# A hybrid decoder step in three-product fp32r: sample tokens' x and B are turned to tokens once, and the sample states of four sequences grow in one group of four matmuls on row strips of TensorE, with some orders beside it rewritten

## The chip, the core and the metric

The kernel runs on one core of a Trainium2 chip. A core has a matrix engine (TensorE, PE in the profile, with PEld for its weight loads), a vector engine (VectorE, DVE), an activation engine (ScalarE, ACT), a general engine (GpSimd, POOL) and a queue engine (SyncE, SP) that here only issues DMAs. Each takes its own list of instructions strictly in order; semaphores tie the lists together. The metric is the device time of one execution in microseconds (us), as a median over runs.

## The reference

One layer of a hybrid decoder works on 256 prompt tokens (one sequence) and 64 sample tokens (eight sequences of eight), 320 columns in all:

```python
h = rms_norm(x, norm_mix_pre);  proj = h @ w_in          # 2048 -> 9248
gate, v   = chunk_spatial_gate(proj[u], proj[v], ...)    # gMLP heads, chunks of 128
xBC       = silu(causal_conv(proj[xBC], conv_state))     # x: 32 heads x 64, B and C: 4 groups x 128
dt        = softplus(proj[dt] + dt_bias); a = -exp(a_log)
# SSD:  h_t = exp(dt_t a) h_{t-1} + dt_t x_t B_t^T,   y_t = h_t C_t  (per head; B, C per group of 8 heads)
x = x + rms_norm([gate || norm(y * silu(z))] @ w_out, norm_mix_post)
up = causal_conv(rms_norm(x, norm_ffn_pre) @ w_up);  g, u = split(up)
x = x + rms_norm((gelu(g) * u) @ w_down, norm_ffn_post)
```

Among the outputs are the SSD states after the step. For each of the eight sample sequences and 32 heads the new state is the old 64 x 128 state times the sequence's total decay plus the sum over its eight tokens of (decay to the end x dt x x) times B. Per sequence and group of eight heads this is a sum over eight tokens that makes 128 x 512 numbers: eight sequences and four groups, 32 such growths.

## The kernel before

**Main work.** Activations lie feature-major (features on partitions, 320 tokens along the row). An fp32 product is made of three fp32r matmuls: activations and weights are each split in a high and a low part, and `accumulate` (L139) adds whi·hi (L141), whi·lo (L142) and wlo·hi (L143) for every 128 x 128 weight block, each 320 columns wide. Weights come in slabs of 1024 columns, 512 KB and eight blocks, 24 matmuls (`slab`, L118): SP loads `wraw` (L124, three buffers), ACT casts it to `whi` (L128, three buffers), DVE subtracts for `wlo` (L130, three buffers). The order of a kernel's time is: input projection with the gMLP and SSD heads between its slabs (to about 806 us), the handover to the FFN, then the FFN in up and down parts.

**Who sets the order.** A scheduler simulates the program and sorts each engine's list by priority. Slabs have high priority. Work beside them is written as Python generators (tasks in the background), which get one step ("tick") for each part of a slab, so that a `yield` moves what follows it by a slab or a part of one. `tc.issue_after(ins)` keeps what stands in it behind a named instruction in the order; it is no wait on the chip beyond the data's own.

**To tokens.** The SSD heads need x and B with tokens on partitions. `by_token` (L382) turns a 128 x 128 piece by a matmul against the identity. For the group's B: `bt_ps`, 16 pieces; for each of four groups' x: `xt_ps`, 16 pieces. Of the four banks of four pieces, two hold the prompt (banks 0, 1). The other two hold sample tokens fourfold: `fourfold` (ACT copies, L390) writes each half of the 64 sample tokens four times side by side, so that the turned piece has them at four places on the partitions. From these DVE makes `xdt` and `xq` (`times`, L800), and ACT sends `xq` to DRAM (`xq_d`). The decay rows `dt` and `dec` have five column groups for this: two for the prompt, one for the 64 samples, two for the fourfold halves (`dt_ps` L473, `dec_ps` L539).

**Growing the sample states** (`renewals`, L1150) runs in the background of the FFN, from 927 to 1318 us. For each group g it loads `xsp` from `xq_d`, splits it, and then goes over i = 0..3: ACT makes `bm`, the B rows masked by `bsel` to one sequence (the other rows zero); two states (h = 0, 1) are loaded, scaled by POOL (`tote`), grown by one matmul of all 128 rows each (`up_ps`, L1202, 512 columns), added by DVE (L1203) and sent out by ACT's queue (L1207). A state's buffer `st` is one of four.

**The handover to the FFN.** After the last slab of the output projection, `rsqrt_by_root` makes the norm's factor `r2b` (`spread`, L290). `x1_ready` (L1034) then makes for each of 16 feature tiles on DVE: scale (L1039), add x (L1040), and the split for the next product, `h_hi` by ACT (L370) and `h_lo` by DVE (L371). PE needs `h_hi` and `h_lo` of tile 0, then of 1, and so on. In the same stretch ACT copies the prompt's final states out of PSUM (L1017, L1044), and POOL adds them (L1162). DVE then sums the squares (`sq3`, L300) for the next norm, and PE turns these to `tsum` (L282).

**The decay masks.** For each head group ACT makes `cs` by a Relu (L896) and an Exp from a row that a DMA spreads (`cs<-dacs_d`, L792); `xs`, the SiLU of the convolved x, is made by ACT too (L428, L429) and is what the transposes `xt_ps` wait for.

Of the kernel before, what the change touches and what calls it, by code (L numbers as in the profile page):

```python
# [34 lines left out]
def hybrid_step(  # L35
# [38 lines left out]
    bsel = cp.tile([P, 4], F32, name="bsel")  # L74
# [4 lines left out]
    def masks():  # L79
# [7 lines left out]
        for r in range(4):  # L87
            rs = slice(32 * r, 32 * r + 32)
            pool.tensor_copy(bsel[rs], bd2[rs, rs].rearrange("p (b t) -> p b t", b=4)[:, :, 0])
# [13 lines left out]
    def col(i):  # L103
        return prm[:, i:i + 1]
# [228 lines left out]
    xq_d = dr.tile([4, P, 2, 512], F32, name="xq_d")  # L333
    bsp_d = dr.tile([P, 2, 512], F32, name="bsp_d")
# [28 lines left out]

    def split(hi, lo, x, scale=None):

        if scale is None:
            act.copy(hi, x)
            dve.tensor_tensor(out=lo, in0=x, in1=hi.bitcast(F32), op=ALU.subtract)
        else:
            made = act.activation(hi, x, AF.Copy, scale=scale).ins  # L370
            dve.scalar_tensor_tensor(out=lo, in0=x, scalar=scale, in1=hi.bitcast(F32), op0=ALU.mult, op1=ALU.subtract)  # L371
            return made
# [13 lines left out]

    def fourfold(out, x):

        for i in range(2):
            act.copy(out[:, :, i], x[:, :, 32 * i:32 * i + 32].unsqueeze(2).to_broadcast([P, 4, 4, 32]))  # L390
        return out.rearrange("p k i q t -> p k (i q t)")

    with ExitStack() as mctx:
# [47 lines left out]
        dt = op.tile([P, 5, NH], F32, name="dt")  # L441
        sda = op.tile([P, 3, NH], F32, name="sda")
        dec = op.tile([P, 5, NH], F32, name="dec")
# [4 lines left out]
        def dt_columns(xf, pre):  # L448
# [15 lines left out]
            for i in range(2):  # L464
                pool.tensor_copy(dtf[:, (3 + i) * P:(4 + i) * P].rearrange("p (q t) -> p q t", q=4),
                                 dtf[:, NP + 32 * i:NP + 32 * i + 32].unsqueeze(1).to_broadcast([P, 4, 32]))

        def steps():
# [3 lines left out]
            for c in range(5):  # L472
                pe.matmul(ps[:, NH * c:NH * c + NH], dtf[:, P * c:P * c + P], heads4, start=True, stop=True)  # L473
            H5 = 5 * NH
            dve.tensor_tensor(out=dt, in0=ps[:, :H5].rearrange("p (c h) -> p c h", c=5),
                              in1=bias_bc.unsqueeze(1).to_broadcast([P, 5, NH]), op=ALU.add)

            e = op.tile([P, 5, NH], F32, name="sp_e")
            q = dec
            z2 = tp.tile([P, NT], F32, tag="pv", name="sp_z2", bufs=4)[:, :5 * NH].rearrange("p (c h) -> p c h", c=5)  # L480
            act.activation(e, dt, AF.Abs)
# [11 lines left out]
            dve.scalar_tensor_tensor(out=dt, in0=dt, scalar=0.0, in1=q, op0=ALU.max, op1=ALU.add)  # L493
# [3 lines left out]
            dve.scalar_tensor_tensor(out=da, in0=dt, scalar=-1.0, in1=ea.unsqueeze(1).to_broadcast([P, 5, NH]),  # L497
# [36 lines left out]
            later_s = tp.tile([P, NT], F32, tag="pv", name="later_s", bufs=4)[:NS, :2 * P].rearrange("p (r q t) -> p r q t", r=2, q=4)  # L534
            for r in range(2):
                rs = slice(32 * r, 32 * r + 32)
                pool.tensor_tensor(out=later_s[:, r], in0=later[:NS, rs].unsqueeze(1).to_broadcast([NS, 4, 32]),
                                   in1=bd[:, rs].unsqueeze(1).to_broadcast([NS, 4, 32]), op=ALU.mult)
                pe.matmul(ps[:, (3 + r) * NH:(4 + r) * NH], later_s[:, r].rearrange("p q t -> p (q t)"), da[:NS, 2],  # L539
                          start=True, stop=True)  # L540
            act.activation(dec.rearrange("p c h -> p (c h)"), ps[:, :H5], AF.Exp)
            dve.tensor_tensor(out=dt[:, 3:5], in0=dt[:, 3:5], in1=dec[:, 3:5], op=ALU.mult)
# [207 lines left out]
        with tc.tile_pool(name="sd", bufs=1) as sd:  # L750
            btok = sd.tile([P, 2, 512], F32, name="btok")

            bsp = sd.tile([P, 2, 512], F32R, name="bsp")
# [4 lines left out]
            x4 = fourfold(sd.tile([P, 4, 2, 4, 32], F32, tag="x4", name="b4", bufs=1), bT[:, :, NP:NT])  # L758
            for c in range(4):
                ps = misc("bt_ps")  # L760
                for g in range(4):
                    by_token(ps[:, P * g:P * g + P], (bT if c < 2 else x4)[:, g], c % 2)
                if c < 2:
                    act.copy(btok[:, c, :], ps)
                else:
                    b = bsp[:, c - 2]
                    act.copy(b, ps)
                    for rs in (slice(32, 64), slice(96, P)):
                        dve.tensor_tensor(out=b[rs], in0=ps[rs], in1=b[rs].bitcast(F32), op=ALU.subtract)
            act.dma_start(bsp_d, bsp.bitcast(F32))  # L770
# [4 lines left out]
            def ssd(g):  # L775
# [26 lines left out]
                x4 = fourfold(sd.tile([P, 4, 2, 4, 32], F32, tag="x4", name="x4", bufs=1), xs[:, :, NP:NT])  # L802
                turned = []
                yield
                for c in range(4):
# [3 lines left out]
                    for j in range(4):  # L809
                        by_token(ps[:, P * j:P * j + P], (xs if c < 2 else x4)[:, j], c % 2)  # L810
                    if c < 2:
                        times(xdt[:, c, :], ps, c)
                    else:
                        turned.append(ps)
                xq = sd.tile([P, 2, 512], F32, tag="x4", name="xq", bufs=1)
# [572 lines left out]
```

## Time and profile before

| what | value |
|---|---|
| median of 3 runs | 1770.68 us (1770.61 to 1771.82) |
| the profiled execution | 1769.41 us |
| its span | 1767.7 us |
| TensorE clock granted | 1.0 of full, every slice |
| PE busy | 1758.7 us (99%), 12207 instructions |
| DVE / ACT / POOL busy | 1163.9 (66%) / 815.9 (46%) / 266.5 us (15%) |
| DMA | 303.35 MB, mean 172 GB/s |

The page lists instructions by line, engine, operation and tile. Matmuls on PE overlap, so a matmul's listed time (310 ns for 320 columns) is longer than the interval at which they follow each other; intervals are read from start to start in the timeline. The chain of work that ended last is traced back from the last instruction. In a row of the timeline, the brackets give the idle time of that engine before the instruction and what ended it.

### The profile page before, as it was taken

The page shows a single profiled execution, that of the slowest core. Times are in us where ns is not written, and L with a number is a line of the kernel's source. Part 1 is how long each engine was busy: PE and PEld are TensorE (multiplying, and loading weights), DVE is VectorE, ACT ScalarE, POOL GpSimd, SP SyncE. Part 2 cuts the span into 40 slices and gives each one's busy share as a digit, 9 for nine tenths or more (in the row PEclk, how much of TensorE's full clock was granted, in tenths as well). Part 3 has the DMA queues.
Part 4 walks back from the last instruction along what each step waited for, and adds up shares of the span by engine and source line. Part 5 has one row for each costly group of instructions (what it writes and reads, how often), then busy time and mean ns, then how long its engine had stood idle before and what let it go on. Part 6 is the DMA issues. An engine that isn't in the chain of part 4 may idle for free.

```text
span 1767.7 us, 31184 instructions
## 1 busy us (share of the span) xinstructions
PE 1758.7 (99%) x12207; PEld 1737.5 (98%) x12207; DVE 1163.9 (66%) x1956; ACT 815.9 (46%) x1201; POOL 266.5 (15%) x596
## 2 busy tenths in 40 slices
PE   9999999999999999999999999999999999999998
PEld 9999999999999999998999999999999999999998
DVE  7349754657767576678865666676767565656575
ACT  7344545333754544445545434343434343333335
POOL 1003210000111001022321312021101010111004
PEclk9999999999999999999999999999999999999999
DMA  7455544445665644444656656556554444444443
GB/s 253 137 179 182 172 156 150 156 155 191 226 210 161 209 144 138 158 161 145 195 177 200 209 177 204 191 184 210 183 180 157 146 156 146 156 152 148 156 147 107
DMA packets 228691, 303.35 MB, mean 172 GB/s; under 512 B 19552, under 2 KB 150720, under 8 KB 228352
## 3 DMA queue, kind: packets, MB, share of 16 engines
q1 hardware_dynamic: 216560, 281.27, 49.7%
q10 hardware_dynamic: 10448, 15.57, 2.4%
q0 software_dynamic: 1536, 4.52, 1.0%
q8 instruction: 96, 1.57, 0.4%
q14 instruction: 51, 0.42, 0.1%
HBM read 283.47 MB, written 17.58 MB: 170 GB/s over the span
## 4 chain that ended last, share of the span: by engine, by line
PE 98%; DVE 1%; DMA 0%; ACT 0%; issue 0%; POOL 0%; DVEq 0%; ACTq 0%
PE ps L141 21%; PE ps L143 21%; PE ps L142 21%; PE pd L141 10%; PE pd L143 10%; PE pd L142 10%; PE y_ps L910 1%; PE yo_ps L859 0%; PE up_ps L1202 0%; PE sg L714 0%; PE tsum L282 0%; PE xt_ps L382 0%; PE vt_ps L599 0%; PE early L70 0%; PE s_ps L841 0%; DMA cs<-dacs_d 0%
## 5 line engine op out<-in xcount | busy, mean ns | idle before, releaser
L130 DVE TENSOR_TENSOR wlo<-wraw,whi 128x1024 fp32r<-128x1024 f32 x470 | 585.5, 1246 | 409.3 <-ACT whi L128 406.8
L128 ACT CAST whi<-wraw 128x1024 fp32r<-128x1024 f32 x470 | 492.3, 1048 | 705.2 <-PE ps L142 432.8
L141 PE MATMUL ps<-h_hi,whi 128*128 128x320 f32 x2528 | 782.7, 310 | 0.5 <-ACT h_hi L370 0.5
L142 PE MATMUL ps<-h_lo,whi 128*128 128x320 f32 x2528 | 780.7, 309 | 1.4 <-DVE h_lo L371 1.4
L143 PE MATMUL ps<-h_hi,wlo 128*128 128x320 f32 x2528 | 779.9, 309 | 0.0
L142 PEld LDWEIGHTS ps<-h_lo,whi 128*128 128x128 f32 x2528 | 475.2, 188 | 2.6 <-DVE h_lo L371 1.9
L141 PEld LDWEIGHTS ps<-h_hi,whi 128*128 128x128 f32 x2528 | 474.9, 188 | 2.6 <-ACT h_hi L370 1.3
L143 PEld LDWEIGHTS ps<-h_hi,wlo 128*128 128x128 f32 x2528 | 474.7, 188 | 0.2
L141 PE MATMUL pd<-fhi,whi 128*128 128x320 f32 x704 | 217.3, 309 | 0.0
L143 PE MATMUL pd<-fhi,wlo 128*128 128x320 f32 x704 | 217.3, 309 | 0.0
L142 PE MATMUL pd<-flo,whi 128*128 128x320 f32 x704 | 217.3, 309 | 0.0
L141 PE MATMUL pd<-ohi,whi 128*128 128x320 f32 x448 | 139.5, 312 | 0.0
L143 PE MATMUL pd<-ohi,wlo 128*128 128x320 f32 x448 | 138.7, 310 | 0.0
L142 PE MATMUL pd<-olo,whi 128*128 128x320 f32 x448 | 138.6, 309 | 0.0
L142 PEld LDWEIGHTS pd<-flo,whi 128*128 128x128 f32 x704 | 132.1, 188 | 0.7
L143 PEld LDWEIGHTS pd<-fhi,wlo 128*128 128x128 f32 x704 | 132.1, 188 | 0.0
L141 PEld LDWEIGHTS pd<-fhi,whi 128*128 128x128 f32 x704 | 132.1, 188 | 0.0
L234 DVE TENSOR_TENSOR acc_ffn<-acc_ffn,pd 128x320 f32<-128x320 f32 x160 | 76.9, 482 | 32.3 <-PE pd L143 31.1
L141 PEld LDWEIGHTS pd<-ohi,whi 128*128 128x128 f32 x448 | 84.0, 188 | 1.9 <-ACT cs L897 0.8
L142 PEld LDWEIGHTS pd<-olo,whi 128*128 128x128 f32 x448 | 84.1, 188 | 0.2 <-issue 0.2
L143 PEld LDWEIGHTS pd<-ohi,wlo 128*128 128x128 f32 x448 | 84.1, 188 | 0.0
L1094 POOL COPY ptf<-pad 128x2 f32<-128x2 f32 x88 | 21.9, 250 | 406.0 <-DVE pad L1082 405.5
(303 smaller groups left out, 1546.5 us busy)
## 6 DMA issues: line engine op xcount, KB each, us to landing
wraw<-in_ffn_w_up SPq DMA_DIRECT2D x176, 512.0 KB, 3.5
wraw<-in_w_in SPq DMA_DIRECT2D x142, 512.0 KB, 3.5
wraw<-in_ffn_w_down SPq DMA_DIRECT2D x88, 512.0 KB, 3.3
wraw<-in_w_out SPq DMA_DIRECT2D x64, 512.0 KB, 3.3
st<-in_state_ssm SPq DMA_DIRECT2D x64, 256.0 KB, 4.5
out_ssm_state_sample<-st ACTq DMA_DIRECT2D x32, 256.0 KB, 2.7
cs<-dacs_d SPq DMA_DIRECT2D x16, 320.0 KB, 5.9
xr<-in_xT SPq DMA_DIRECT2D x4, 640.0 KB, 5.3
```

Of the source, the lines that this page charges most:

```text
L128: act.copy(hi[:, :m], raw[:, :m])
L130: dve.tensor_tensor(out=lo[:, :m], in0=raw[:, :m], in1=hi[:, :m].bitcast(F32), op=ALU.subtract)
L141: pe.matmul(ps, whi, xhi, start=first, stop=False)
L142: pe.matmul(ps, whi, xlo, start=False, stop=False)
L143: newest[0] = pe.matmul(ps, wlo, xhi, start=False, stop=last).ins
L234: dve.tensor_tensor(out=acc[:, nb, :], in0=acc[:, nb, :], in1=ps[:, :NT], op=ALU.add)
L910: pe.matmul(ps[64 * i:64 * i + 64, cols], w(hl), x(hl, m, cpx), tile_position=(0, 64 * i), **flags)
L1094: pool.tensor_copy(ptf[:, k, :], pad[:, 256:258])
```

## The change

1. **To tokens once.** `fourfold` and its buffers are gone. Samples' B and x are turned once: of the third bank, B in four pieces 64 tokens wide, x in two pieces 128 tokens wide (the last 128 columns, for tokens on the upper partitions) and two 64 wide; the fourth bank is gone. The result goes to one DRAM array `xb_d` (x and B of the 64 tokens, per group).
2. **Fewer decay rows.** `dt` has three turned groups where there were five, `dec` four; the matmul for the fourfold rows (L539) is one where it was two.
3. **Row strips.** Per group, 16 small DMAs bring each sequence's eight tokens of x and B to four places in a strip of 32 partitions (`tokens`). ACT copies the rounded high parts, and DVE makes the low parts by two masked operations with `low` (a constant of -1 and 0, made at the start in place of `bsel`). A strip thus holds hi·hi, hi·lo, lo·hi and lo·lo of eight tokens. Four matmuls then stand in a row, each on 32 rows of the array at `tile_position=(32*i, 0)` and each into a PSUM bank of its own: four sequences' states. Two such groups (h = 0, 1) per g, eight in all. States are loaded four at once; those of h = 1 lie in buffers `s1` and `x1d` that the SSD part has left.
4. **Relu later.** The decay masks' Relu stands behind the last SiLU (`issue_after(last_silu)`); in group 2 the transposes come one tick later.
5. **The handover.** In `x1_ready`, scale, add and split have an order of their own, so that `h_lo` of tile 0 stands before the work of later tiles; POOL's adds of the final states (and their outputs) stand behind a small POOL copy that reads the last tile of x1.

```diff
-            x4 = fourfold(sd.tile([P, 4, 2, 4, 32], F32, tag="x4", name="b4", bufs=1), bT[:, :, NP:NT])
-            for c in range(4):
+            for c in range(3):
                 ps = misc("bt_ps")
+                n = P if c < 2 else NS
                 for g in range(4):
-                    by_token(ps[:, P * g:P * g + P], (bT if c < 2 else x4)[:, g], c % 2)
+                    pe.transpose(ps[:n, P * g:P * g + P], bT[:, g, P * c:P * c + n], ident)
...
-                x4 = fourfold(sd.tile([P, 4, 2, 4, 32], F32, tag="x4", name="x4", bufs=1), xs[:, :, NP:NT])
-                turned = []
-                yield
-                for c in range(4):
+                yield from repeat(None, 2 if g == 2 else 1)
+                for c in range(3):
...
-                        by_token(ps[:, P * j:P * j + P], (xs if c < 2 else x4)[:, j], c % 2)
+                        if c < 2:
+                            by_token(ps[:, P * j:P * j + P], xs[:, j], c)
+                        else:
+                            n = P if j < 2 else NS
+                            pe.transpose(ps[:n, P * j:P * j + P], xs[:, j, NT - n:NT], ident)
...
-            for c in range(5):
+            for c in range(3):
                 pe.matmul(ps[:, NH * c:NH * c + NH], dtf[:, P * c:P * c + P], heads4, start=True, stop=True)
...
-                pe.matmul(ps[:, (3 + r) * NH:(4 + r) * NH], later_s[:, r].rearrange("p q t -> p (q t)"), da[:NS, 2],
-                          start=True, stop=True)
...
+            pe.matmul(ps[:, 3 * NH:4 * NH], later_s.rearrange("p r t -> p (r t)"), da[:NS, 2], start=True, stop=True)
...
                     for c, (o, n) in enumerate(at):
-                        act.activation(m[:, o:o + n], m[:, o:o + n], AF.Relu, bias=sda[:, c, h0 + hl:h0 + hl + 1], scale=-1.0)
+                        with tc.issue_after(last_silu):
+                            act.activation(m[:, o:o + n], m[:, o:o + n], AF.Relu, bias=sda[:, c, h0 + hl:h0 + hl + 1], scale=-1.0)
...
-                    with first() if kt < 2 else tc.high_priority(offset=100000), tc.issue_after(added[0] if kt else behind):
-                        dve.scalar_tensor_tensor(out=a, in0=a, scalar=col(prm_at["norm"][0] + kt), in1=r2b, op0=ALU.mult, op1=ALU.mult)
-                        added.append(dve.tensor_tensor(out=a, in0=a, in1=xr[q][:, k, :], op=ALU.add).ins)
-                        whole.append(split(hT[0][:, kt, :], hT[1][:, kt, :], a, col(prm_at["norm"][1] + kt)))
+                    with first() if kt < 2 else tc.high_priority(offset=100000):
+                        with tc.issue_after(behind if kt == 0 else added[0] if kt == 1 else lower[low0]):
+                            dve.scalar_tensor_tensor(out=a, in0=a, scalar=col(prm_at["norm"][0] + kt), in1=r2b, op0=ALU.mult, op1=ALU.mult)
+                        with tc.issue_after(lower[low0] if kt else behind):
+                            added.append(dve.tensor_tensor(out=a, in0=a, in1=xr[q][:, k, :], op=ALU.add).ins)
+                        with tc.issue_after(added[0]):
+                            whole.append(split(hT[0][:, kt, :], hT[1][:, kt, :], a, col(prm_at["norm"][1] + kt)))
...
+            after_v.append(pool.tensor_copy(there, x1[:, KD - 1, 0:1]).ins)
             for g, s1, x1d, _ in rest:
...
-                with tc.issue_after(whole[KD - 1]):
+                with tc.issue_after(after_v[-1]):
                     pool.tensor_tensor(out=s1, in0=s1, in1=x1d, op=ALU.add)
...
+            def tokens(g):
+                rows = xb_d[g].rearrange("(h i t) c -> i t h c", h=2, i=4)
+                for i in range(4):
+                    for r in range(4):
+                        at = 32 * i + TS * r
+                        sp.dma_start(raw[at:at + TS], rows[i])
...
+                act.copy(part, raw)
+                yield
+                for at, m in ((slice(0, 512), 0), (slice(512, 640), 1)):
+                    dve.scalar_tensor_tensor(out=part[:, :, at], in0=part[:, :, at].bitcast(F32), scalar=low[:, m:m + 1], in1=raw[:, :, at],
+                                             op0=ALU.mult, op1=ALU.add)
...
+                    if h == 0:
+                        ahead.append(load(g, 1))
+                    elif g < 3:
+                        ahead.append(load(g + 1, 0))
+                        tokens(g + 1)
+                    yield from repeat(None, 2)
+                    grown = [misc("up_ps") for _ in range(4)]
+                    for i in range(4):
+                        at = slice(32 * i, 32 * i + 32)
+                        pe.matmul(grown[i], part[at, h, 512:], part[at, h, :512], start=True, stop=True, tile_position=(32 * i, 0))
+                    for i in range(4):
+                        dve.tensor_tensor(out=st[i], in0=st[i], in1=grown[i], op=ALU.add)
+                        yield
+                        act.dma_start(o_ssm_s[4 * h + i, g], st[i])
```

**PE in the FFN.** `ps` and `pd` are banks of the up and down products; `fhi`, `flo` are the FFN's gated activations. Before, the first growth stands between the end of an up part and a down part:

```order
L141 MATMUL ps_3_9921<-h_hi,whi 128x320
L142 MATMUL ps_3_9921<-h_lo,whi 128x320
L143 MATMUL ps_3_9921<-h_hi,wlo 128x320
L1202 MATMUL up_ps<-xsp,kept 128x512
L141 MATMUL pd_0_10251<-fhi,whi 128x320
L142 MATMUL pd_0_10251<-flo,whi 128x320
L143 MATMUL pd_0_10251<-fhi,wlo 128x320
```

The second group of the changed kernel, between two blocks of an up part:

```order
L143 MATMUL ps_3_10508<-h_hi,whi 128x320
L144 MATMUL ps_3_10508<-h_lo,whi 128x320
L145 MATMUL ps_3_10508<-h_hi,wlo 128x320
L1203 MATMUL up_ps<-xb_parts 128x512 x4
L143 MATMUL ps_0_10505<-h_hi,whi 128x320
L144 MATMUL ps_0_10505<-h_lo,whi 128x320
L145 MATMUL ps_0_10505<-h_hi,wlo 128x320
```

A single matmul of 128 rows stood at each of 32 places; now four of 32 rows stand together at each of eight.

**DVE at the handover.** The rows begin with the last step of the norm's factor (`rs_r`). Before:

```order
L268 SCALAR_TENSOR_TENSOR rs_r<-rs_v,rs_r 128x3
L1039 SCALAR_TENSOR_TENSOR acc_mix<-acc_mix,prm,spread 128x320
L1040 TENSOR_TENSOR acc_mix<-acc_mix,xr 128x320
L1039 SCALAR_TENSOR_TENSOR acc_mix<-acc_mix,prm,spread 128x320 x2
L1040 TENSOR_TENSOR acc_mix<-acc_mix,xr 128x320
L371 SCALAR_TENSOR_TENSOR h_lo<-acc_mix,prm,h_hi 128x320
L1039 SCALAR_TENSOR_TENSOR acc_mix<-acc_mix,prm,spread 128x320
L371 SCALAR_TENSOR_TENSOR h_lo<-acc_mix,prm,h_hi 128x320
```

Changed:

```order
L270 SCALAR_TENSOR_TENSOR rs_r<-rs_v,rs_r 128x3
L1031 SCALAR_TENSOR_TENSOR acc_mix<-acc_mix,prm,spread 128x320
L1033 TENSOR_TENSOR acc_mix<-acc_mix,xr 128x320
L1031 SCALAR_TENSOR_TENSOR acc_mix<-acc_mix,prm,spread 128x320
L374 SCALAR_TENSOR_TENSOR h_lo<-acc_mix,prm,h_hi 128x320
L1033 TENSOR_TENSOR acc_mix<-acc_mix,xr 128x320
L1031 SCALAR_TENSOR_TENSOR acc_mix<-acc_mix,prm,spread 128x320 x2
L374 SCALAR_TENSOR_TENSOR h_lo<-acc_mix,prm,h_hi 128x320
```

Between the first add and the first `h_lo` stand one operation now, three before.

**SP in the FFN.** Weight slabs (`wraw`) and the growths' loads share SP's list. Before, from a down part to an up part:

```order
L124 DMA wraw_10423<-in_ffn_w_down 128x4x256
L1169 DMA st_10457<-in_state_ssm 128x512
L124 DMA wraw_10464<-in_ffn_w_down 128x4x256
L1169 DMA st_10458<-in_state_ssm 128x512
L124 DMA wraw_10501<-in_ffn_w_down 128x4x256
L124 DMA wraw_10546<-in_ffn_w_up 128x2x512
```

Changed, where the states of g = 1, h = 0 are loaded and its tokens (`xb`) begin:

```order
L1163 DMA st_10570<-in_state_ssm 128x512
L126 DMA wraw_10624<-in_ffn_w_up 128x2x512
L1163 DMA st_10571<-in_state_ssm 128x512
L1163 DMA st_10572<-in_state_ssm 128x512
L126 DMA wraw_10663<-in_ffn_w_up 128x2x512
L1163 DMA st_10573<-in_state_ssm 128x512
L1172 DMA xb_9591<-xb_d_97 8x2x640
L126 DMA wraw_10695<-in_ffn_w_up 128x2x512
```

Four state loads stand within three slabs where two stood within two, and token loads follow.

135 lines of the change are left out of this document (51 added, 84 removed).

## Prediction

> **What bounds the kernel now.** I read the page first, then the waits of PE, then the chain and the timeline where PE stood. The page:
>
> ```profile
> span 1767.7 us, 31184 instructions
> PE 1758.7 (99%) x12207; PEld 1737.5 (98%) x12207; DVE 1163.9 (66%) x1956; ACT 815.9 (46%) x1201; POOL 266.5 (15%) x596
> ...
> PEclk9999999999999999999999999999999999999999
> ...
> PE 98%; DVE 1%; DMA 0%; ACT 0%; issue 0%; POOL 0%; DVEq 0%; ACTq 0%
> ```
>
> PE is the bound from end to end, with its clock granted in every slice. So the time is a sum of PE's instructions, from start to start, and of the few places where PE waits:
>
> ```profile
> PE ps L142 <- DVE h_lo L371: 1.4, 2, 1.2
> PE xt_ps L382 <- ACT xs L428: 1.2, 1, 1.2
> PE early L70 <- DVE ones L66: 1.1, 1, 1.1
> PE ps L141 <- ACT h_hi L370: 0.5, 1, 0.5
> ```
>
> (Total us, times, longest.) The start cannot go; the other three are 3.1 us. What the change can gain is therefore small in advance: PE work that it takes away, these waits, and no more. What it can lose has no such limit. The main work's rate is seen here:
>
> ```profile
> 562.40 0.31 PE L143 MATMUL pd<-ohi,wlo 128*128 128x320 f32 x1
> ...
> 562.84 0.31 PE L143 MATMUL pd<-ohi,wlo 128*128 128x320 f32 x1
> ```
>
> Three matmuls take 0.44 us, a slab of 24 takes 3.52. This part is untouched.
>
> The sum is made against the profiled execution, 1769.41 us, of which the span is 1767.7 and 1.7 lie around it. The median shown, 1770.68, is 1.27 above it; I add that at the end.
>
> **1. Transposes.** B had 16 and each of four groups' x had 16; now 12 each. 20 are gone.
>
> ```profile
> 423.49 0.87 PE bt_ps L382 x8
> ...
> 431.57 0.87 PE xt_ps L382 x8
> ```
>
> 0.87 / 8 = 0.109 us each, with no wait inside: 20 x 0.109 = **−2.2 us**. Twelve of the rest are 64 tokens wide now. I take no gain for these, since a transpose row of that width is not there; if they cost half, 12 x 0.05 = −0.6, which goes into the range. The ACT copies of `fourfold`, and DVE's larger products for the fourfold rows, go off engines that PE does not wait for here, so they count nothing; ACT becomes free earlier ahead of its `xs`.
>
> **2. Decay rows.** 4 of 10 records of `dt_ps` and 2 of 4 of the fourfold `dec_ps` go:
>
> ```profile
> 205.25 1.03 PE dt_ps L473 x10
> ...
> 247.46 0.56 PE dec_ps L539 x4
> ```
>
> 1.03 x 4/10 + 0.56 x 2/4 = **−0.7 us**. The DVE and POOL work that shrinks with them is beside slabs. The constant `low` (three DVE operations in place of four POOL copies) is made ahead of the first slabs' work on DVE; its cost is below 0.3 us if PE saw it, and PE's one wait there ends with `ones`, which stands ahead of it: 0.
>
> **3. The growths.** A growth now stands between main matmuls as one that covers the array:
>
> ```profile
> 1060.23 0.39 PE L1202 MATMUL up_ps<-xsp,kept 128*128 128x512 f32 x1
> ...
> 1060.46 0.31 PE L141 MATMUL ps<-h_hi,whi 128*128 128x320 f32 x1
> ```
>
> It takes 0.23 us from its start to the next start, 0.92 for four, and there are 32 of them:
>
> ```profile
> L1202 PE MATMUL up_ps<-xsp,kept x32: 387/393/398, 927.4 to 1318.4; 128*128 128x512 f32 x32
> ```
>
> The new group has four with the same 512 columns and a quarter of the rows. The trace shows no row strips. The nearest are column strips, of which the SSD part has four beside each other:
>
> ```profile
> 463.04 1.93 PE L859 MATMUL yo_ps<-st,cb_cms 128*32 128x256 f32 x32
> 464.91 0.41 PE L141 MATMUL pd<-ohi,whi 128*128 128x320 f32 x1
> 465.16 0.31 PE L142 MATMUL pd<-olo,whi 128*128 128x320 f32 x1
> ...
> 482.47 0.31 PE L143 MATMUL pd<-ohi,wlo 128*128 128x320 f32 x1
> 482.71 0.66 PE L910 MATMUL y_ps<-cs,xdt 128*64 128x128 f32 x8
> ...
> 809.11 1.88 PE L933 MATMUL fin_ps<-x1d,btok 128*128 128x512 f32 x4
> ```
>
> A strip's record of 256 columns follows the last after (464.91 − 463.04) / 32 = 0.058 us, where a record of 512 columns on the whole array in the same type takes 1.88 / 4 = 0.47, so 256 would take 0.235: four column strips do overlap four times over. But going in and out of strips costs: the first main matmul after the strips takes 0.25 us to the next start and not 0.147 (464.91 to 465.16), and a start of strips comes 0.24 after a main one (482.47 to 482.71), 0.1 late; 0.2 together. So:
> - all four at once: 0.23 + 0.2 = 0.43 per group, 8 x (0.43 − 0.92) = −4.0;
> - no overlap: 0.92 + 0.2 = 1.12, +1.6;
> - four weight loads of 128 columns one after the other, at 0.109 as the transposes (which load as many columns and do little else): 0.23 + 3 x 0.109 + 0.2 = 0.76, −1.3.
>
> I take each strip to start 0.058 after the last, the interval that strips have shown: 0.23 + 3 x 0.058 + 0.2 = 0.60, 8 x (0.60 − 0.92) = **−2.5 us**, with −4.0 and +1.6 as the ends.
>
> The Trainium skill's page "TensorE: Matmul & The Clock Gate", section "Measured speedup vs the span model", gives 3.07 times for four row strips of 32 rows and 512 columns. By it a group would take 0.92 / 3.07 = 0.30 us, with the 0.2 around it 0.50, an estimate that makes −3.4 of this term and 1762.4 of the whole. No row of this trace has row strips to test it.
>
> What the growths need: 16 `bm` and 8 `xsp` operations on ACT become four copies, DVE's subtractions become masked ones; both beside slabs. DVE's adds stand four in a row now, 4 x 0.69 us = 2.8. Cover:
>
> ```profile
> L1203 DVE TENSOR_TENSOR st<-st,up_ps x32: 674/686/690, 930.3 to 1318.9; 128x512 f32<-128x512 f32 x32
> ...
> 1057.60 1.23 DVE L130 TENSOR_TENSOR wlo<-wraw,whi 128x1024 fp32r<-128x1024 f32 x1
> ...
> 1058.85 0.37 SPq L124 DMA_DIRECT2D wraw<-in_ffn_w_up  x1
> ...
> 1060.33 1.05 ACT L128 CAST whi<-wraw 128x1024 fp32r<-128x1024 f32 x1 [2.76 <-PE ps L142]
> ```
>
> The cast waits for PE to free one of three `whi`, so its slab is needed two slabs (7.0 us) later; cast and `wlo` take 2.3 of that. 4.7 us are left, and the adds' 2.8 fit: 0. Four PSUM banks are needed at once; the last group's have long been emptied, since groups stand many slabs apart.
>
> **4. Relu and `xs`.** PE's wait at `xt_ps`:
>
> ```profile
> 568.74 1.17 ACT L896 ACTIVATE cs<-cs,sda 128x128 f32<-128x128 f32 x4 [1.43 <-DMA cs<-dacs_d]
> 569.82 0.40 ACT L428 ACTIVATE xs<-cv 128x256 f32<-128x256 f32 x1
> 570.27 0.76 PE L382 MATMUL xt_ps<-ident,xs 128*128 128x128 f32 x5 [1.16 <-ACT xs L428]
> ```
>
> ACT stood 1.43 us for a DMA at the Relu, then did 1.17 us of Relu, with the last `xs` behind both. Now the Relu stands behind `xs`, and group 2's transposes come a tick later. So the wait goes: **−1.2 us** (0 if the masks now are late for `y_ps`). Queued behind the waiting Relu now are casts; their cover is the 4.7 us above against 1.43 + 1.17.
>
> **5. The handover.**
>
> ```profile
> 809.21 1.27 POOL L1162 TENSOR_TENSOR s<-s,x1d 128x512 f32<-128x512 f32 x1 [6.46 <-ACT x1d L1017]
> ...
> 809.89 0.93 DVE L1040 TENSOR_TENSOR acc_mix<-acc_mix,xr 128x320 f32<-128x320 f32 x1
> ...
> 811.66 0.48 DVE L1040 TENSOR_TENSOR acc_mix<-acc_mix,xr 128x320 f32<-128x320 f32 x1
> 811.97 2.80 POOL L1162 TENSOR_TENSOR s<-s,x1d 128x512 f32<-128x512 f32 x2 [1.49 <-ACT x1d L1044]
> 812.07 1.56 DVE L371 SCALAR_TENSOR_TENSOR h_lo<-acc_mix,prm,h_hi 128x320 fp32r<-128x320 f32 x1
> ...
> 813.68 0.42 PE L142 MATMUL ps<-h_lo,whi 128*128 128x320 f32 x1 [1.21 <-DVE h_lo L371]
> ```
>
> The same DVE add takes 0.93 us while POOL adds, 0.48 while it does not; `h_lo` takes 1.56. With POOL's adds moved away, `h_hi` of tile 0 comes 0.45 earlier; with one operation ahead of it in place of three, `h_lo` of tile 0 is done at about 811.6 (add to 810.4, then scale and ACT's part to 811.0, then 0.5), not 813.6. PE would be up to 2.1 us ahead. What is late next is `tsum`, which waits for DVE's last square:
>
> ```profile
> 853.64 2.27 DVE L300 TENSOR_TENSOR sq<-sq,sq 128x320 f32<-128x320 f32 x4
> ...
> 856.07 0.79 PE tsum L282 x6
> ```
>
> DVE ends at 855.91, PE starts `tsum` at 856.07: there is no slack now, and the changed order puts the last square behind one more `wlo`, 1.2 us. I keep **−0.9** of the 2.1, with 0 and −2.1 as ends. POOL's own list stands behind the new copy until x1 is whole; what waits there are the FFN's first paddings, which come after x1 in any case.
>
> **Sum:** −2.2 − 0.7 − 2.5 − 1.2 − 0.9 = −7.4 (unrounded). 1769.4 − 7.4 = 1762.0 profiled, and 1.27 more for the median: **1763.3**. The best ends together make −10.7, 1760.0. 0.2% of the time, about what a measurement of this kernel can tell from no change, is 3.5 us: 1767.1 to 1774.2.
>
> **Rivals.**
>
> A. *SP stands at the state loads, and weights come late; slower.* Loads for g + 1, h = 0 go into buffers of h = 0 of g, and stand in SP's list ahead of slabs (at three places). If SP gets there as the adds begin, it waits for four adds and an output's landing:
>
> ```profile
> wraw<-in_ffn_w_up SPq DMA_DIRECT2D x176, 512.0 KB, 3.5
> ...
> out_ssm_state_sample<-st ACTq DMA_DIRECT2D x32, 256.0 KB, 2.7
> ```
>
> 2.8 + 2.7 = 5.5 us. A slab load is issued as a `wlo` ends (1058.85), lands 3.5 us later, and is cast third in turn from 1060.33, at 1067.4: 5.0 us of slack there, and 4.7 to PE, 9.7. So 5.5 is covered. It decides against the change from where SP stands 13.3 us at each of the three places: 3.6 past the slack, 10.9 in all, which eats the 7.4 and 3.5 more: 1774.2. The 52 more DMAs on SP (64 small token loads for 12 larger ones), many with a slab behind them, are what could lengthen it. Time then 1775 or more; chance 0.12.
>
> B. *The strips do not overlap.* The growths cost +1.6 in place of −2.5: 1767.4. For it: no row strip is in the trace. Against it: column strips overlap. Chance 0.11, about half on each side of 1767.1.
>
> C. *All strips at once, and the handover kept whole.* −4.0 and −2.1: 1760.6. For it: the fourfold overlap of column strips; against it: `tsum` has no slack. Chance 0.08.
>
> D. *Only the work that is taken off PE counts*: waits come back elsewhere (the masks late for `y_ps`, `tsum` late), and strips gain nothing: −2.9, 1767.8. Chance 0.09, mostly within 0.2%.
>
> My forecast has the remaining 0.60, at 1761 to 1766. Faster by over 0.2%: 0.60 + 0.08 + 0.05 + 0.02 = 0.75. Within: 0.06 + 0.07 = 0.13. Slower: 0.12. The range 1759.5 to 1768.8 takes in B, C and D and the narrow transposes, and leaves out A.
>
> **What would show it.** In the changed profile: eight groups of four `up_ps`, each group about 0.6 us from its first start to the next main start but one interval (step 3; near 1.1 is B); no PE wait for `xs` in group 2 (step 4); PE's first `h_lo` matmul less than 0.5 us after its `h_hi` ones end, and a wait at `tsum` of about 1.3 (step 5); 12 transposes per group at 0.109 or less (step 1). I would be wrong if PE waits in the FFN for `whi` or `wlo`, which it does not do once now; SP's waits at `st` would then say why (A).

## The result, and the profile after

The changed kernel takes 1763.86 us (median of five runs, 1762.61 to 1764.40), the kernel before 1770.61 (five runs, 1769.55 to 1771.82): a ratio of 0.9964, with a 95% interval of 0.9953 to 0.9975. Forecast were 1763.3, and 1759.5 to 1768.8. The profiled execution of the changed kernel took 1764.01 us, 0.15 above its median; that of the kernel before was 1.20 below this median. So the profiles differ by less (1767.7 − 1762.3 = 5.4 us of span) than the medians (6.75). Line numbers have moved by a few: L141, L142, L143 are now L143, L144, L145, and `wlo` is L132.

The changed kernel's page, and PE's waits (total us, times, longest):

```profile
span 1762.3 us, 31116 instructions
PE 1752.8 (99%) x12181; PEld 1729.9 (98%) x12181; DVE 1154.0 (65%) x1947; ACT 806.5 (46%) x1172; POOL 277.3 (16%) x590
...
PE 98%; DVE 1%; DMA 1%; ACT 0%; issue 0%; SPq 0%; DVEq 0%; ACTq 0%
```

```profile
PE ps L145 <- DVE wlo L132: 1.9, 1, 1.9
PE early L70 <- DVE ones L66: 1.1, 1, 1.1
PE tsum L284 <- DVE sq L302: 0.4, 1, 0.4
PE ps L143 <- ACT whi L130: 0.4, 1, 0.4
PE tsum L284 <- DVE acc_mix L601: 0.3, 1, 0.3
```

The waits for `xs` (1.2), `h_hi` (0.5) and `h_lo` (1.4) are gone. A wait of 1.9 us for a weight slab's low part has come in their place, and three smaller ones: two at `tsum`, and one for a `whi` in the first 100 us.

Where the 5.4 us lie is read from three places that both programs pass in the same order. The chain of the kernel before, and of the changed one, at the start of the sums before the handover, at the next `tsum` behind it, and at the last norm:

```profile
805.61 1.95 PE tsum L282 x18
...
856.07 0.79 PE tsum L282 x6
...
1751.74 0.74 PE tsum L282 x6
```

```profile
800.50 1.95 PE tsum L284 x18
...
852.63 0.80 PE tsum L284 x6
...
1745.83 0.74 PE tsum L284 x6
```

| stretch | before | after | difference | forecast |
|---|---|---|---|---|
| start to the sums before the handover | 805.61 | 800.50 | −5.1 | −4.1 (steps 1, 2, 4) |
| from there to `tsum` of the FFN's norm | 50.46 | 52.13 | +1.7 | −0.9 (step 5) |
| from there to the last norm | 895.67 | 893.20 | −2.5 | −2.5 (step 3) |
| from there to the end | 15.96 | 16.47 | +0.5 | 0 |
| span | 1767.7 | 1762.3 | −5.4 | −7.4 |

The first and the third stretch came as forecast or better; the end came 0.5 late, and why stays open. The handover, which should have gained, lost.

How firm the first row is shows in the runs told below. From a `tsum` that both pass at 30 us to the sums before the handover, the changed kernel and the eight variants of it that leave this part alone take 769.93 to 769.95 us, and the kernel before 775.31: −5.4. The first 30 us differ more: 30.56 to 31.50 among the same nine runs, 30.30 before.

This is PE in the handover, with DVE and POOL, in the timeline of the changed kernel:

```profile
831.04 1.22 DVE L132 TENSOR_TENSOR wlo<-wraw,whi 128x1024 fp32r<-128x1024 f32 x1
832.17 5.05 DVE L374 SCALAR_TENSOR_TENSOR h_lo<-acc_mix,prm,h_hi 128x320 fp32r<-128x320 f32 x4
832.26 4.62 POOL L1155 TENSOR_TENSOR s<-s,x1d 128x512 f32<-128x512 f32 x3
...
837.15 2.35 DVE L132 TENSOR_TENSOR wlo<-wraw,whi 128x1024 fp32r<-128x1024 f32 x2
...
838.42 0.41 PE L145 MATMUL ps<-h_hi,wlo 128*128 128x320 f32 x1 [1.94 <-DVE wlo L132]
```

Four `h_lo` took 1.93 us in the kernel before (at 838.27) and 5.05 here, in the same 4.6 us in which POOL now adds the final states. The next `wlo` comes 3.1 us later for it, and PE waits 1.94. The theory from this: POOL's adds slow DVE wherever they stand; the change has moved them from the start of the handover to its end, and has not put them where DVE has time. The rival: the new order of DVE's work, or late slab loads, make the wait.

### The profile page after: what moved, and what is told of

It reads as the page before. It is cut to its first block, busy times and chain, and to the rows that moved or that the text cites. A ratio compares the mean times of both kernels' runs of the same rounds, so it can differ in the third digit from the quotient of the medians.

```text
span 1762.3 us, 31116 instructions
## 1 busy us (share of the span) xinstructions
PE 1752.8 (99%) x12181; PEld 1729.9 (98%) x12181; DVE 1154.0 (65%) x1947; ACT 806.5 (46%) x1172; POOL 277.3 (16%) x590
## 4 chain that ended last, share of the span: by engine, by line
PE 98%; DVE 1%; DMA 1%; ACT 0%; issue 0%; SPq 0%; DVEq 0%; ACTq 0%
PE ps L143 21%; PE ps L145 21%; PE ps L144 21%; PE pd L143 10%; PE pd L145 10%; PE pd L144 10%; PE y_ps L900 1%; DMA wraw<-in_ffn_w_up 0%; PE yo_ps L848 0%; PE sg L705 0%; PE tsum L284 0%; PE vt_ps L590 0%; DVE wlo L132 0%; ACT whi L130 0%; PE xt_ps L385 0%; PE up_ps L1203 0%
## 5 line engine op out<-in xcount | busy, mean ns | idle before, releaser
L132 DVE TENSOR_TENSOR wlo<-wraw,whi 128x1024 fp32r<-128x1024 f32 x470 | 581.3, 1237 | 438.8 <-ACT whi L130 434.9
L143 PE MATMUL ps<-h_hi,whi 128*128 128x320 f32 x2528 | 782.4, 310 | 0.4 <-ACT whi L130 0.4
L145 PE MATMUL ps<-h_hi,wlo 128*128 128x320 f32 x2528 | 777.6, 309 | 1.9 <-DVE wlo L132 1.9
L144 PE MATMUL ps<-h_lo,whi 128*128 128x320 f32 x2528 | 779.4, 309 | 0.0
L143 PEld LDWEIGHTS ps<-h_hi,whi 128*128 128x128 f32 x2528 | 474.6, 188 | 4.3 <-issue 2.8
L145 PEld LDWEIGHTS ps<-h_hi,wlo 128*128 128x128 f32 x2528 | 474.0, 188 | 2.5 <-DVE wlo L132 2.4
L144 PEld LDWEIGHTS ps<-h_lo,whi 128*128 128x128 f32 x2528 | 474.8, 188 | 0.0
L143 PE MATMUL pd<-fhi,whi 128*128 128x320 f32 x704 | 217.3, 309 | 0.0
L145 PE MATMUL pd<-fhi,wlo 128*128 128x320 f32 x704 | 216.9, 308 | 0.0
L144 PE MATMUL pd<-flo,whi 128*128 128x320 f32 x704 | 216.9, 308 | 0.0
L143 PE MATMUL pd<-ohi,whi 128*128 128x320 f32 x448 | 139.5, 312 | 0.0
L145 PE MATMUL pd<-ohi,wlo 128*128 128x320 f32 x448 | 138.5, 309 | 0.0
L144 PE MATMUL pd<-olo,whi 128*128 128x320 f32 x448 | 138.5, 309 | 0.0
L143 PEld LDWEIGHTS pd<-fhi,whi 128*128 128x128 f32 x704 | 132.1, 188 | 1.0 <-issue 1.0
L144 PEld LDWEIGHTS pd<-flo,whi 128*128 128x128 f32 x704 | 132.1, 188 | 0.0
L145 PEld LDWEIGHTS pd<-fhi,wlo 128*128 128x128 f32 x704 | 132.1, 188 | 0.0
L143 PEld LDWEIGHTS pd<-ohi,whi 128*128 128x128 f32 x448 | 84.0, 188 | 1.4 <-issue 0.7
L144 PEld LDWEIGHTS pd<-olo,whi 128*128 128x128 f32 x448 | 84.1, 188 | 0.2 <-issue 0.2
L145 PEld LDWEIGHTS pd<-ohi,wlo 128*128 128x128 f32 x448 | 84.1, 188 | 0.0
```

Of the source, the lines that this page charges most:

```text
L132: dve.tensor_tensor(out=lo[:, :m], in0=raw[:, :m], in1=hi[:, :m].bitcast(F32), op=ALU.subtract)
L143: pe.matmul(ps, whi, xhi, start=first, stop=False)
L144: pe.matmul(ps, whi, xlo, start=False, stop=False)
L145: newest[0] = pe.matmul(ps, wlo, xhi, start=False, stop=last).ins
```

## The experiments

**Short adds.** The changed kernel, every engine's order as it is:

```diff
-                    pool.tensor_tensor(out=s1, in0=s1, in1=x1d, op=ALU.add)
+                    pool.tensor_tensor(out=s1[:, 0:16], in0=s1[:, 0:16], in1=x1d[:, 0:16], op=ALU.add)
```

> The changed kernel with POOL's three adds of the final states cut from 512 columns to 16 (480 columns of each are left out, so those outputs lack their last term); every engine's order stays as it is. Theory (POOL's adds slow DVE's h_lo at 832 to 837, and that makes PE's 1.94 us wait at 838): DVE's four h_lo take about 2.0 us in place of 5.05, PE's wait at wlo is gone and the one at tsum shrinks; 1.9 to 2.5 us faster than the changed kernel, median about 1761.6. Rival (the DVE order or late weight loads make the wait): the wait stays at 1.5 us or more, median 1763.9.

Median 1762.61 (1761.21 to 1763.36). DVE's row, and PE's first two waits:

```profile
832.06 1.94 DVE L374 SCALAR_TENSOR_TENSOR h_lo<-acc_mix,prm,h_hi 128x320 fp32r<-128x320 f32 x4
```

```profile
PE tsum L284 <- DVE sq L302: 1.5, 1, 1.5
PE early L70 <- DVE ones L66: 1.1, 1, 1.1
```

The four `h_lo` take 1.94 with the same instructions in the same order, and the wait at `wlo` is gone: the cause of that wait is shown. The size was a miss: 1.25 us won by medians, not 1.9 to 2.5. PE reaches `tsum` earlier and now waits 1.5 there for DVE's last square, where it waited 0.4.

The handover stretch (sums to `tsum`) is 49.57, 0.9 less than in the kernel before, which is what step 5 had forecast. It is 2.6 less than the changed kernel's 52.13, but a part of that is the clock: the changed kernel's profiled run had half the clock for 3.4 us there (last section). Two kernels told below have the same handover, and their runs kept the full clock. The first of them, with group 2's tick undone:

```profile
801.30 1.95 PE tsum L284 x18
...
852.05 0.79 PE tsum L284 x6
```

That is 50.75; the second, with Relu and tick undone, has 51.23. So the adds cost 1.2 to 1.7 us here, in keeping with the 1.25 of the medians, and the lower clock goes with the other 0.9 to 1.4.

**Adds behind the norm's factor; adds at 880.** The small copy that POOL waits on reads something later:

```diff
-            after_v.append(pool.tensor_copy(there, x1[:, KD - 1, 0:1]).ins)
+            after_v.append(pool.tensor_copy(there, r3[:, 0:1]).ins)                         # first kernel
+            after_v.append(pool.tensor_copy(there, nxt[0][:, 3, 0:1].bitcast(F32)).ins)     # second kernel
```

> The changed kernel with POOL's small copy reading r3 (the factor of the FFN's norm, ready near 856 us) in place of the last tile of x1, so that the three adds stand behind tsum. Theory: the wait at wlo is gone as with short adds; the adds now slow DVE's pad products near 857, where there is slack; median 1761.6 to 1762.2, which would beat the changed kernel. Rival (order or loads): 1763.9. A third way: the contention comes back as a PE wait after 857: 1763 to 1764.5.

> The changed kernel with POOL's small copy reading the last tile of the first gated activations (about 880 us), so that the three adds stand where DVE has slack. Theory (POOL's adds cost wherever DVE is what PE waits for, and nothing elsewhere): no PE wait at wlo near 838 nor at pad near 857, a wait of 0.5 to 1.5 at tsum stays; 0.6 to 1.1 us faster than with the adds at 855, median 1761.0 to 1761.6. Rival (the wait of 1.1 at pad comes from elsewhere): 1762.0 as with the adds at 855, or slower if the later adds hold state loads back on SP.

The first: 1761.99 (1761.76 to 1762.70). The second: 1761.22 (1760.77 to 1762.27), 0.9947 of the kernel before (0.9933 to 0.9961). PE's waits of the first:

```profile
PE ps L143 <- DVE pad L1077: 1.1, 1, 1.1
PE early L70 <- DVE ones L66: 1.1, 1, 1.1
PE tsum L284 <- DVE sq L302: 0.5, 1, 0.5
```

With the adds at 855 the wait at `wlo` is gone and one of 1.1 stands at `pad`, where DVE empties the banks that PE needs next. DVE is slowed there too (three `gcv` take 2.55 us, 1.53 with the adds at 880), but the longest step is another. POOL's own copies (`stg`) queue among its adds, and ACT stands 3.55 us at the sending of one:

```profile
862.85 1.28 ACT L1090 ACT_TABLE_LOAD   x1 [3.55 <-POOL stg L1087]
```

So ACT's next `whi` comes late, DVE waits 1.89 for it, and empties the bank behind it. With the adds at 880 the wait at `pad` is gone, and `tsum` waits 0.2; DVE stands idle there through all three adds:

```profile
879.47 3.77 POOL L1155 TENSOR_TENSOR s<-s,x1d 128x512 f32<-128x512 f32 x3
...
883.57 4.91 DVE L132 TENSOR_TENSOR wlo<-wraw,whi 128x1024 fp32r<-128x1024 f32 x3 [4.11 <-ACT whi L130]
```

The stretches: handover 48.58 and 48.26; FFN 894.83 and 893.59, where short adds have 893.20. So the adds cost something at three places, and at the fourth little: 0.4 in the FFN, of which 0.3 is a wait at `up_ps`, where POOL's scaling of the states (L1191) now meets DVE's `xb_parts` (1.28 us for its 256 columns, 0.48 in the changed kernel).

**Adds early, with the new DVE order; old order, with the late adds.** The first takes the small copy out; the second puts the old three lines back in `x1_ready`:

```diff
-            after_v.append(pool.tensor_copy(there, x1[:, KD - 1, 0:1]).ins)
-                with tc.issue_after(after_v[-1]):
+                with tc.issue_after(whole[KD - 1]):
```

> The changed kernel without the small copy: POOL's adds stand again at the handover, where they stood before the change, with the new DVE order kept. Theory: DVE's first add and h_lo are slowed again (0.9 and 1.0 to 1.5 us in place of 0.5), PE waits 1 to 1.9 us in sum between 804 and 810, and the wait at 838 is gone; median 1763 to 1764.5. Rival (order or loads make the wait at 838): both waits, 1765 or more.

> The changed kernel with the old order of scale, add and split in x1_ready; the small copy and the late adds stay. Theory: h_lo of tile 0 comes about 1 us later, PE waits about 0.8 to 1.1 us at the handover and so much less at 838, since DVE's slow stretch there is set by x1 and not by PE: median 1763.5 to 1764.3, the new order alone is worth next to nothing. Rival (the new order is what makes the wait at 838): the wait there is gone, median 1762.9 or less.

Early adds: 1765.15, and the runs scatter (ten runs, 1762.31 to 1767.74). Old order: 1764.87 (1763.54 to 1765.48). In the first, DVE's first add takes 0.93 again, PE waits 1.0 in two pieces for `h_hi`, and no longer at `wlo`; so far as forecast. But `tsum` waits 2.6 us, which was not, and the clock falls behind it. The chain that leads to this `tsum` begins at a slab load of 6.45 us. The slab loads on the chain to `tsum` with early adds, in the changed kernel (two), and with the adds at 880:

```profile
833.55 6.45 DMA wraw<-in_ffn_w_up
```

```profile
833.15 4.18 DMA wraw<-in_ffn_w_up
...
838.43 4.62 DMA wraw<-in_ffn_w_up
```

```profile
835.14 3.64 DMA wraw<-in_ffn_w_up
```

With early adds, with short ones and in the changed kernel, the outputs of the final states and loads of sample states stand beside these slab loads (in the changed kernel six state loads from 834 to 850). Both stand behind the adds, so with the adds at 880 they come from 871 us on. The 1.3 us by which that handover is shorter than the one with short adds (48.26, 49.57) may be these DMAs and not the adds. So late slab loads, the rival, do not make the wait at `wlo`, but they have a part in the wait at `tsum`; no run moves them alone.

In the second of the two kernels, the first `h_lo` makes PE wait 0.18 only, not 0.8 to 1.1, and the wait at `wlo` is 2.35: with POOL out of the way the old order is nearly as good at the start, and what is won there is waited out at 838. The new order is worth 1.0 by medians whose runs overlap, between nothing and 1 us; whether it is worth anything is not settled.

**Relu and tick.** Three kernels undo the Relu's place, group 2's later tick, and both:

```diff
-                        with tc.issue_after(last_silu):
-                            act.activation(m[:, o:o + n], m[:, o:o + n], AF.Relu, bias=sda[:, c, h0 + hl:h0 + hl + 1], scale=-1.0)
+                        act.activation(m[:, o:o + n], m[:, o:o + n], AF.Relu, bias=sda[:, c, h0 + hl:h0 + hl + 1], scale=-1.0)
...
-                yield from repeat(None, 2 if g == 2 else 1)
+                yield from repeat(None, 1)
```

> The changed kernel with the decay masks' Relu again ahead of the last SiLU; the tick that moves group 2's transposes back stays. Theory (the moved Relu took the wait of 1.16 us away): PE waits for xs before group 2's transposes again, up to 1.2, median 1764.5 to 1765.1. Rival (the tick alone covers it, since the transposes stand a slab later): no such wait, median 1763.9.

> The changed kernel with group 2's transposes where they stood; the Relu stays behind the last SiLU. Theory: xs is ready, a PE wait of at most 0.3, median 1763.9 to 1764.2. Rival (only the tick took the wait away): a wait near 1, median 1764.8 or more.

> Both undone. Either theory: the wait of about 1.2 us at group 2's transposes is back, median about 1765.1. If it is not, something else in the change had taken it away (the copies of the fourfold rows that ACT no longer makes), and median 1763.9.

1764.07 (1763.78 to 1764.53), 1764.15 (1763.47 to 1765.39), and 1765.52 (1764.88 to 1766.42), against 1763.86. Only with both undone does PE wait, in the timeline of that kernel:

```profile
569.38 0.77 PE L385 MATMUL xt_ps<-ident,xs 128*128 128x128 f32 x5 [1.40 <-ACT xs L425]
```

With the Relu alone undone the transposes start at 569.20 without a wait: a slab of 3.5 us stands ahead of them. With the tick alone undone they wait 0.20. Each of the two covers the wait by itself, and the pair is worth 1.7 by medians. From the `tsum` of 30 us to the sums, the stretch that takes 769.94 in the changed kernel, the three take 769.94, 770.34 and 771.57: nothing, 0.4 and 1.6. That the moved Relu was needed, as the first expectation had it, fell.

**The strips.** Each group's four matmuls are issued twice, in turn or in pairs, or with half their columns:

```diff
-                    for i in range(4):
+                    for i in (0, 1, 2, 3, 0, 1, 2, 3):      # in turn
+                    for i in (0, 0, 1, 1, 2, 2, 3, 3):      # in pairs
                         at = slice(32 * i, 32 * i + 32)
-                        pe.matmul(grown[i], part[at, h, 512:], part[at, h, :512], start=True, stop=True, tile_position=(32 * i, 0))
+                        pe.matmul(grown[i][:, :256], part[at, h, 512:], part[at, h, :256], start=True, stop=True, tile_position=(32 * i, 0))   # half columns
```

> The changed kernel with each group's four strip matmuls issued twice in turn (strips 0 1 2 3 0 1 2 3; the second round writes the same numbers again). A group of four took 0.435 us from its first start to the next main start. M0 (all four stream beside each other, 0.23, and 0.2 is a fixed price of going in and out): a second round adds 0.23, group 0.66. M1 (a strip matmul takes a slot of 0.109, as a transpose does, whatever it streams): 8 x 0.109 = 0.87. M2 (strips share the stream, each taking half of 0.23): 0.87 to 0.92. B (no overlap): 1.84.

> The same eight matmuls with each strip's two next to each other (0 0 1 1 2 2 3 3). M0 and M1: the second on a strip waits for the first to stream 0.23, other strips go on beside: a group takes 1.0 to 1.4 us, more than in turn. M2: no strip waits for itself more than for another, 0.87 to 0.92 as in turn. No overlap: 1.84.

> The changed kernel with 256 of the 512 columns in each strip matmul and in DVE's add behind it (half of the sample states' growth is left out). M0: 0.115 + 0.2 = 0.32 per group. M1 (a slot of 0.109 per matmul): 0.435, unchanged. M2 (shared stream): 0.22 to 0.25.

One run each: 1765.77, 1766.58 and 1763.18. The first two do the same work twice over, and the third leaves half of the states' growth out, in DVE's adds too. What tells is the group's row in the chain (from its first start to the next main start; a chain row names as many records as carry the chain). The changed kernel, in turn, in pairs, half columns:

```profile
1016.91 0.44 PE up_ps L1203 x4
1017.34 0.34 PE pd L143
```

```profile
966.67 0.67 PE up_ps L1203 x8
```

```profile
1053.70 0.68 PE up_ps L1203 x7
```

```profile
1016.85 0.32 PE up_ps L1203 x4
```

A second round adds 0.67 − 0.435 = 0.23 (the changed kernel's eight groups show 0.43 or 0.44), what one matmul of 512 columns takes on the whole array; half the columns take 0.115 less. The eight groups of each kernel agree within 0.01, and the FFN stretch differs from the changed kernel's by +1.76, +1.99 and −1.14: +0.22, +0.25 and −0.14 per group. So four strips do stream fully beside each other, and the group's other 0.2 is fixed. This is M0; M1, M2 and no overlap are out. The paired order should have been slower by M0 and M1 and was not: a strip's second matmul does not hold up the next strip's first.

**The best of it.** The adds at 880, and the three DVE operations that make `low` moved into `renewals`, so that in DVE's list they stand a little later, behind the sum that the `tsum` of 30 us reads:

```diff
-        dve.tensor_reduce(out=low[:, 0:1], in_=d4[:, :, 2:4], axis=mybir.AxisListType.XYZ, op=ALU.add)
...
             with tc.issue_after(slab_load[-1]):
+                dve.tensor_reduce(out=low[:, 0:1], in_=d4[:, :, 2:4], axis=mybir.AxisListType.XYZ, op=ALU.add)
...
                 sp.dma_start(tote, tote_d)
```

> The kernel with the adds at 880, and the three DVE operations that make the constant low moved from the first rows of DVE's list to behind the sum that tsum waits for at 30 us. Theory (these operations make PE's wait of 0.3 at that tsum, which the kernel before does not have): the wait is gone, 0.2 to 0.3 faster, median about 1761.0. Rival: the wait is of another cause and stays, 1761.2.

1760.76 (1760.14 to 1762.04), 0.9944 of the kernel before (0.9931 to 0.9956). PE's longest waits:

```profile
PE early L70 <- DVE ones L66: 1.1, 1, 1.1
PE ps L140 <- DVE wlo L127: 0.3, 2, 0.2
PE up_ps L1203 <- DVE xb_parts L1186: 0.3, 1, 0.3
```

The wait at the `tsum` of 30 us is gone, so `low` made it, by the order of DVE's list: with it, two masks (`upper_s`, 0.51 us) had come to stand ahead of the sum, at 29.9, and without it they are done at 12.9. Over the kernel with the adds at 880 alone this is 0.46 by medians, within the runs' scatter; over the changed kernel the two together are 3.1.

## Why the prediction was right

The time was right within 0.6 us, but not by all of its terms: two errors of about 2.6 and 1 us had opposite signs, and the span fell by 2.0 less than forecast while the medians hid 1.35 of that. So near a hit is luck; the mechanisms of steps 1 to 4 hold, with what is said of them here, and step 5 failed.

*Step 1, transposes: right.* The chain of the changed kernel has

```profile
423.01 0.87 PE bt_ps L752 x8
425.79 0.44 PE bt_ps L752 x4
...
434.88 0.44 PE xt_ps L800 x4
```

Four of the 64-wide kind take 0.44, 0.11 each: the narrow ones save nothing, as taken. 20 x 0.109 = 2.2 has gone.

*Step 2, decay rows: right.* `dt_ps` takes 0.59 (1.03 before), the fourfold `dec_ps` 0.34 (0.56): −0.66 for −0.69. "Its cost is 0" for `low` was wrong by 0.3: the last experiment shows it.

*Step 4, Relu and `xs`: the size right and a little low, the reason half right.* The wait is gone, and the undone pair costs 1.7 by medians. But either edit would have done.

The rest of the −5.1, about 0.6 (0.9 with the 0.3 of `low` set against it), is what I had no term for: main matmuls after each inserted bundle start late by about 0.09, and there are fewer bundles; some short waits in group 3 went too (before, about 0.4 behind the eight transposes at 671). This is read from the rows and was not tried by itself.

*Step 3, the growths: right in size, 0.64 for 0.60, by luck.* A group with its surroundings, in the timeline of the changed kernel:

```profile
966.68 0.31 PE L145 MATMUL ps<-h_hi,wlo 128*128 128x320 f32 x1
966.92 0.51 PE L1203 MATMUL up_ps<-xb_parts 32*128 32x512 f32 x4
967.36 0.41 PE L143 MATMUL ps<-h_hi,whi 128*128 128x320 f32 x1
967.61 0.31 PE L144 MATMUL ps<-h_lo,whi 128*128 128x320 f32 x1
```

From 966.68 to 967.61 two main intervals (0.293) and the group: 0.93 − 0.293 = 0.637, and 8 x (0.637 − 0.92) = −2.3 of the measured −2.5. The parts were wrong, and their errors cancel: strips do not start 0.058 apart (0.17 for three), they stream together, and the price of going in and out is 0.2 within and 0.2 around, twice what the forecast took. The Trainium skill's page "TensorE: Matmul & The Clock Gate", section "Measured speedup vs the span model", gives 3.07 times for such a four, from which the forecast had its estimate of 0.30 us. The row gives 0.435 to the next main start, so 0.92 / 0.435 = 2.1 times and not 3.07 here, where full-array matmuls stand on both sides of a single round; a second round took 0.23, which is four times.

*Step 5, the handover: wrong, by 2.6 us.* The step that failed is "With POOL's adds moved away": they were moved on DVE's path again. Of the 2.6, 1.2 to 1.7 is what the adds cost (52.13 is the run with the lower clock, 50.75 and 51.23 those without, 49.57 the short adds), and the rest goes with the clock, which no step had a term for. With the adds short the step came as worked out: no wait for `h_lo`, 1.5 at `tsum` where 1.3 was forecast, and −0.9. The first half held (`h_lo` of tile 0 was done at 806.6, 2.3 us behind the start of the first scale at 804.3; before, 4.3 us), and so did "what is late next is `tsum`", but before `tsum` came the slow `h_lo` at 832, which I had named only as POOL's list standing behind x1, without asking what DVE does beside the adds when they come. The forecast had this as its sign of being wrong, "if PE waits in the FFN for `whi` or `wlo`"; the wait came, but by POOL and not by SP's state loads, the cause it had named. The trace of before had the row that prices it: the same adds took DVE's add from 0.48 to 0.93.

*The rivals.* A did not come: SP waited 7.9 us in four pieces at the state loads, the longest 5.2 where 5.5 was the bound, and no slab was late for it. B is out by the strips' runs. C was half of it: the strips do overlap, though at twice its price for going in and out, and the handover did not keep its gain. Of D, one half came: a wait came back (at `wlo`), but the strips gained.

## What to carry

A slow helper that is moved off one critical stretch must be followed to where it lands: name what the neighbouring engine does there, and price it from the row in which the two last met. Strips of the array pay when several rounds stand in a row, since going in and out cost 0.4 us here and a round 0.23. And a median that agrees is no proof of the terms: compare stretches between places that both programs pass.

## What was unexpected

**POOL's adds took DVE to less than half its rate.** Three adds of 512 columns, 4.62 us, took four `h_lo` from 1.94 to 5.05. The adds were slower too: with DVE idle they took 3.77. The Trainium skill's page "GPSIMD Engine Reference", section "1. Specifications", says that this engine shares its SBUF interfaces with VectorE and contends with DVE instructions that have two SBUF inputs. The trace agrees, 3.1 us for 4.6 us of adds.

**The granted clock halves for 3.4 or 6.8 us in some executions and not in others.** The changed kernel's profiled run, in windows just behind the sums (length, then busy time by engine; the third number from the right is the granted clock):

```profile
802.50:804.50 2.00, 1.75 (x6) 0.88 (x6) 0.96 (x6) 0.88 (x3) 0.00 (x0) 0.85 0.00 0
804.50:806.50 2.00, 2.00 (x3) 0.67 (x2) 1.80 (x4) 1.02 (x2) 0.00 (x0) 0.50 0.00 0
806.50:808.50 2.00, 2.00 (x10) 1.42 (x9) 2.00 (x6) 1.28 (x3) 0.00 (x0) 0.80 0.00 0
```

The three windows lose 0.15, 0.50 and 0.20 of 2 us each, 1.7 in all, which is 3.4 us at half the clock. The kernel before has 1.00 in all windows at that place, in its one profiled run; of the thirteen profiled runs of changed kernels, the one above, the Relu alone undone, and the strips twice in turn and in pairs have this dip. In the kernel with early adds it follows PE's wait of 2.57 us at `tsum`:

```profile
852.87 1.41 PE L284 MATMUL tsum<-ones,sq 128*128 128x1 f32 x6 [2.57 <-DVE sq L302]
854.14 0.61 PE L144 MATMUL ps_one<-h_lo,whi 128*128 128x320 f32 x1
854.55 0.47 PE L145 MATMUL ps_one<-h_hi,wlo 128*128 128x320 f32 x1
854.82 0.47 PE L143 MATMUL ps_one<-h_hi,whi 128*128 128x320 f32 x1
```

Main matmuls come 0.267 apart there and not 0.147, until 859.6, twice 3.4 us; its FFN stretch is 896.3 where the changed kernel has 893.2. With the old order a wait of 2.35 at 837, and with half the columns one of 2.4, brought a dip of 3.4 us too; a wait of 2.4 with the tick undone and one of 2.5 with both undone brought none. So of five stalls of 2.35 to 2.57 us, two cost themselves alone, and three 1.7 or 3.4 us of clock besides. The Trainium skill's page "TensorE: Matmul & The Clock Gate", in "What's actually happening", tells of a free-running window of 3.4 us of activity that sets the clock. That the same stall sometimes brings a dip agrees with a window that does not start with the stall, and the dips of 3.4 us, or twice that, agree with its length; but the waits that did it here are shorter than the 3.4 us of idleness that the Trainium skill's page asks for. No run here varied the length of a wait alone.

**A strip's queue.** Eight strip matmuls take the same time in turn and in pairs (0.67, 0.68), so what a strip has yet to stream does not hold up a matmul for another strip that stands behind it.
